# Feed-forward weights of a hybrid layer: split ahead of the stage, loaded two pairs ahead, with no pool border in between

## The chip, the cores and the metric

The kernel runs on one core of a Trainium2 chip. The metric is the time of one execution on the device, in microseconds; the figure of a kernel is the median over its runs. Five engines work side by side, each through its own instructions in order: TensorE (PE in the profile) does the matmuls, VectorE (DVE) and ScalarE (ACT) do elementwise work, GpSimd (POOL) little here, and SyncE (SP) issues nearly all transfers from device memory. An instruction starts when the one before it on its engine lets it and when the semaphores that it waits for have come.

## The reference, cut to what matters

The layer has a mixer (a gated delta rule and a differential attention), a cross attention to a memory, and a feed-forward stage. The change touches the end of the cross attention (its output projection) and the feed-forward stage:

```python
h = h + _mem_attn(_rmsnorm(h, p['ln_mem_q']), mem_k, mem_v, p['w_mem_q'], p['w_mem_o'])
hn = _rmsnorm(h, p['ln_ffn'])
h = h + jnp.square(jax.nn.relu(hn @ p['w_ff1'])) @ p['w_ff2']
...
y_prompt = _rmsnorm(hp, ln_final)
y_sample = _rmsnorm(hs, ln_final)
```

D_MODEL is 1024, D_FF is 4096, all in float32. The two request groups have 512 and 64 tokens, which the kernel carries side by side as T = 576 columns.

## The kernel before

**Number format.** Activations lie transposed: features on the 128 partitions, tokens along the row. A float32 factor is kept as a high part (a cast on ScalarE) and a low part (source minus high part, on VectorE), and a product takes three matmuls: high by high, high by low, low by high. `halves_to` (L1220) makes the two parts of an activation, `split_weights` (L155) and `split` (L1279) those of a weight tile. The splits of weights stand under a higher priority, so the scheduler puts them early in each engine's order.

**The output projection of the cross attention.** The loop at L1244 goes over the eight blocks of 128 output features in the order 0, 4, 1, 5, 2, 6, 3, 7. For a block it loads 128 columns of `w_mem_o` into a buffer `raw` (three of them), makes `wh` and `wl` (two of each), and `project` (L169) runs two halves of the tokens, 256 and 320 columns, each into a PSUM bank `pr` (three of them). `add_residual` (L1087) adds the bank to the residual `hT`, and squares it on ScalarE and adds the square to `accq` on VectorE for the norm of the next stage. After each block `combine` (L1224) scales the residual by the gain of the feed-forward norm and forms sums and differences of token halves and of the blocks m and m+4.

**The feed-forward stage.** The norm's factor is taken out of the product (the relu is homogeneous, the square makes it a factor of the second product's result), so the stage works on unnormalized features, and the factor `rB` is applied at the end. The first product is done in 16 pairs of 128-column blocks by a scheme with seven half-size products instead of eight: `ff1_pair` (L1294) loads a pair's weights as two tiles of 512 KB, forms four sums of them on VectorE (L1306, L1307, L1310, L1311), splits them (`a1`, `w12`, `a2`, `w34`, one buffer of each) and runs products 1, 5, 6, 2, 7, 3 and 4, each 12 matmuls of 288 columns, in PSUM banks `ba`, `gs` and `g1`. Products share banks: `keep` (L1342) copies a bank on ScalarE before the next product adds to it, and `put` (L1347) adds two products, takes relu and square and splits the result. Group g is two pairs; beside them run the eight blocks of the second product for group g-1, whose weights `w2` come in tiles of 256 KB. In the last group `last_weights` (L1397) loads and splits the weights of the last eight blocks in four tiles.

**What sets the order.** A scheduler orders each engine's instructions by priority and by when it expects a buffer to be free. Memory comes from pools with a fixed number of buffers for a name. After the loop at L1244 ten matmuls against a column of ones sum `accq` over the features (the norm), the pools `sp` and `wp` of all stages before are closed at L1254, and a new pool `fp` for the feed-forward stage is laid out in the memory that they leave (L1268). A buffer of `fp` waits for the tiles that lay there before.

## Time and profile before

| what | value |
|---|---|
| three runs | 1034.03, 1034.13 and 1035.53 us; median 1034.13 us |
| the profiled execution | 1033.64 us, of which 1031.9 us are the span from its first to its last instruction |
| PE busy | 1001.4 us, 97% of the span, in 6630 matmuls |
| PE's weight loads | 920.4 us, beside the matmuls |
| DVE busy | 701.0 us, 68% |
| ACT busy | 534.9 us, 52% |
| POOL busy | 56.8 us, 6% |
| read and written in device memory | 79.14 MB and 9.74 MB, 86 GB/s over the span |

The page divides the span into 40 slices; in its rows for PE nearly every slice has a 9, that is, 90% or more. The stretch that the change is about lies between 560 us (the end of the cross attention) and 650 us (the second group's start), and the feed-forward stage fills the rest, to 1000 us. [...]

### The profile page before, as it was taken

What the parts mean: (1) busy time and instruction counts of PE and PEld (TensorE: products, weight loads), DVE (VectorE), ACT (ScalarE), POOL (GpSimd) and SP (SyncE); (2) the same over time, 40 slices, a digit from 0 to 9 for tenths busy, and PEclk for the clock granted to TensorE, in tenths of its full rate; (3) what the DMA queues carried; (4) which work ended last, traced back from release to release, by engine and by line L of the source; (5) the groups of instructions that cost most, each with busy time, mean ns of one, the idle gap of its engine ahead of it and who ended that gap; (6) DMA issues with size and microseconds to landing.
All of it is one profiled execution on the core that took longest, in us unless ns stands there. A gap on an engine that the chain in (4) does not pass through costs nothing.

```text
span 1031.9 us, 17262 instructions
## 1 busy us (share of the span) xinstructions
PE 1001.4 (97%) x6630; PEld 920.4 (89%) x6630; DVE 701.0 (68%) x1511; ACT 534.9 (52%) x1152; POOL 56.8 (6%) x123
## 2 busy tenths in 40 slices
PE   9999999999999999999999998999999999999986
PEld 7989899998888877999997888999999999999976
DVE  6676784776666676565665778866666676777783
ACT  6654664333465665444454556754444545555434
POOL 3431010100000000000000000000000000000000
PEclk9999999999999999999999998999999999999999
DMA  7432320100322355523111304222323322222102
GB/s 216 129 100 85 109 60 25 39 21 22 104 67 65 121 175 182 165 83 110 55 42 42 103 1 143 92 86 89 93 83 93 101 83 83 82 83 83 53 30 92
DMA packets 121253, 89.98 MB, mean 87 GB/s; under 512 B 5506, under 2 KB 112128, under 8 KB 120660
## 3 DMA queue, kind: packets, MB, share of 16 engines
q1 hardware_dynamic: 120804, 88.24, 28.4%
q8 instruction: 52, 0.85, 0.3%
q10 hardware_dynamic: 368, 0.66, 0.2%
q14 instruction: 29, 0.24, 0.1%
HBM read 79.14 MB, written 9.74 MB: 86 GB/s over the span
## 4 chain that ended last, share of the span: by engine, by line
PE 77%; DVE 8%; DMA 4%; issue 3%; ACT 3%; POOL 2%; POOLq 0%; ACTq 0%; DVEq 0%; SPq 0%
PE pr L107 42%; PE g L107 14%; PE ba L107 9%; PE gs L107 8%; DMA r<-in_w_ff_dram 3%; PE ba L113 2%; PE g L113 2%; DVE w34l L1284 1%; DVE a2l L1284 1%; ACT w34h L1283 1%; DVE s L1307 1%; DVE s L1306 0%; DVE w2l L1284 0%; DVE wl L162 0%; DVE s L1310 0%
## 5 line engine op out<-in xcount | busy, mean ns | idle before, releaser
L107 PE MATMUL pr<-u,wh 128*128 128x320 f32 (+2 forms) x1240 | 328.3, 342 | 2.0 <-DVE p L323 1.1
L107 PE MATMUL pr<-u,wl 128*128 128x256 f32 (+1 forms) x816 | 227.9, 303 | 0.0
L107 PEld LDWEIGHTS pr<-u,wh 128*128 128x128 f32 x1240 | 211.5, 188 | 18.2 <-DVE p L323 1.3
L107 PEld LDWEIGHTS pr<-u,wl 128*128 128x128 f32 x816 | 149.3, 188 | 3.8 <-issue 0.7
L162 DVE TENSOR_TENSOR wl<-raw,wh 128x1024 fp32r<-128x1024 f32 x65 | 79.6, 1224 | 36.5 <-ACT wh L161 34.7
L107 PE MATMUL pr<-u,w2h 128*128 128x320 f32 (+1 forms) x384 | 97.4, 338 | 4.5 <-DVE u L1389 2.2
L161 ACT CAST wh<-raw 128x1024 fp32r<-128x1024 f32 x65 | 68.3, 1051 | 58.5 <-PE pr L107 52.7
L1283 ACT CAST w2h<-r 128x512 fp32r<-128x512 f32 x56 | 34.7, 621 | 95.1 <-PE pr L107 94.2
L107 PE MATMUL pr<-f,w2h 128*128 128x320 f32 (+1 forms) x288 | 73.2, 338 | 0.9 <-DVE u L1389 0.8
L107 PEld LDWEIGHTS pr<-u,w2h 128*128 128x128 f32 x384 | 64.9, 188 | 10.0 <-issue 4.0
L107 PE MATMUL pr<-u,w2l 128*128 128x256 f32 (+1 forms) x256 | 64.9, 294 | 0.0
L107 PEld LDWEIGHTS pr<-f,w2h 128*128 128x128 f32 x288 | 48.9, 188 | 5.5 <-issue 2.3
L107 PE MATMUL pr<-f,w2l 128*128 128x256 f32 (+1 forms) x192 | 48.7, 294 | 0.0
L107 PEld LDWEIGHTS pr<-u,w2l 128*128 128x128 f32 x256 | 46.9, 188 | 1.3
L1389 DVE TENSOR_TENSOR u<-u,pr 128x256 f32<-128x256 f32 x96 | 40.5, 451 | 10.6 <-PE pr L107 10.2
L208 POOL TENSOR_TENSOR tiny<-tiny,nhalf 128x1 f32<-128x1 f32 (+4 forms) x10 | 10.0, 1003 | 639.2 <-DVE tiny L1453 547.2
L1284 DVE TENSOR_TENSOR w12l<-s,w12h 128x1024 fp32r<-128x1024 f32 x16 | 19.6, 1225 | 35.7 <-ACT w12h L1283 35.7
L1284 DVE TENSOR_TENSOR w2l<-r,w2h 128x512 fp32r<-128x512 f32 x56 | 38.6, 689 | 7.1 <-ACT w2h L1283 6.9
L107 PE MATMUL pr<-wh,u 128*128 128x512 f32 x128 | 41.3, 402 | 0.0
L107 PEld LDWEIGHTS pr<-f,w2l 128*128 128x128 f32 x192 | 35.1, 188 | 1.1
L1092 DVE TENSOR_TENSOR u<-u,pr 128x256 f32<-128x256 f32 (+1 forms) x48 | 21.6, 453 | 19.9 <-PE pr L107 19.8
L457 DVE SCALAR_TENSOR_TENSOR p<-p,gcol,p 128x579 f32<-128x579 f32 x33 | 27.1, 822 | 9.0 <-ACT p L455 8.6
(454 smaller groups left out, 2283.8 us busy)
## 6 DMA issues: line engine op xcount, KB each, us to landing
r<-in_w_ff_dram SPq DMA_DIRECT2D x36, 512.0 KB
raw<-in_w_in_dram SPq DMA_DIRECT2D x28, 512.0 KB
r<-in_w_ff_dram SPq DMA_DIRECT2D x56, 256.0 KB
raw<-in_w_mem_k_dram SPq DMA_DIRECT2D x8, 512.0 KB
raw<-in_w_mem_v_dram SPq DMA_DIRECT2D x8, 512.0 KB
raw<-in_w_out_dram SPq DMA_DIRECT2D x8, 512.0 KB
raw<-in_w_mem_q_dram SPq DMA_DIRECT2D x8, 512.0 KB
raw<-in_w_mem_o_dram SPq DMA_DIRECT2D x8, 512.0 KB
```

The source lines that it names most:

```text
L107: i = nc.tensor.matmul(out, lhsT, rhs, start=start, stop=stop, skip_group_check=skip_group_check)
L113: i = nc.tensor.transpose(out, in_, ident[:n, :n])
L161: A.copy(wh, raw)
L162: V.tensor_tensor(wl, raw, wh.bitcast(F32), ALU.subtract)
L208: G.tensor_tensor(out, in_, bc(nhalf[: in_.shape[0], 0:1], list(in_.shape)), ALU.pow)
L457: V.scalar_tensor_tensor(yv[:, :n], cb[:, i : i + n], cwt[:, m, i : i + 1], yv[:, :n], ALU.mult, ALU.add)
L1092: V.tensor_tensor(hm, hm, b, ALU.add)
L1283: A.copy(wh, src)
L1284: V.tensor_tensor(wl, src, wh.bitcast(F32), ALU.subtract)
L1307: V.tensor_tensor(s12[:, 1], s12[:, 0], A11, ALU.subtract)
L1389: V.tensor_tensor(am, am, b, ALU.add)
```

## The change

The pool `sp` is closed ahead of the output projection's loop and `fp` opened there; `wp` moves to the outer level and stays open to the end. The scaled features and their sums, which lay in four names of `sp`, lie in one tile `mid` of `fp` now. The two first-product tiles of pair 0 are loaded after the fourth block of the loop and split between the other blocks (`split_first`); those of pair 1 are loaded after the loop. From then on `ff1_pair` of pair p ends with the split of pair p+1 and the load of pair p+2. The sums of weights overwrite the loaded tile instead of going to tiles of their own; the split tiles live under the names `wh`, `wl` and `w4`, one set of each, with other groupings than before: `wh` twice for products 1 and 5, one pair of `wl` for products 6 and 7, three `w4` for products 2 and 4 and for product 3. The loaded tiles share the three `raw` buffers with `w_mem_o` and with the four last loads. Squares and their sum move out of the loop into group 2 (some of the squares are scheduled earlier), and the norm's matmuls into group 3.

The multiplications on PE stay the same in number and shape. VectorE and ScalarE each have 18 instructions more, as splits of 1024 columns are divided into splits of 512.

```diff
-    wp = work.enter_context(tc.tile_pool(name="wp", bufs=2))
+    wp = ctx.enter_context(tc.tile_pool(name="wp", bufs=2))
...
+    work.close()
+    fp = ctx.enter_context(tc.tile_pool(name="fp", bufs=1, reuse_waits="tile"))
+    def ft(tag, shape, bufs, dt=F32):
+        return fp.tile(shape, dt, tag=tag, name=nm(tag), bufs=bufs)
+    mid = ft("f1", [P, 8, T], 1)
...
-        scaled[m] = x = small("kd" if m < 4 else "aT", [P, T])
+        k = m % 4
+        scaled[m] = x = mid[:, (0 if m < 4 else 4) + k % 2]
...
+        t12, t34 = (mid[:, i + k % 2].rearrange("p (j n) -> p j n", j=2) for i in (2, 6))
...
-    for m in (0, 4, 1, 5, 2, 6, 3, 7):
-        project(weights(w_mem_o[0], m * P), mo, add_residual(m, True))
+    def wtile(tag, shape, dt=F32R):
+        return wp.tile(shape, dt, tag=tag, name=nm(tag), bufs=3 if tag == "raw" else 2)
+    def load_pair(p):
+        raws[p] = raw = [wtile("raw", raw_, F32) for i in range(2)]
+        for i in range(2):
+            src = w_ff1[0, 512 * i : 512 * i + 512, 2 * P * p : 2 * P * (p + 1)]
+            nc.sync.dma_start(raw[i], src.rearrange("(k p) n -> p k n", p=P))
+    def split_pair(p):
+        a, b = raws.pop(p)
+        A11, A21, A12 = a[:, :, :P], a[:, :, P:], b[:, :, :P]
+        s1 = ft("s1", block_, 2)
+        parts[p] = ws = {}
+        with tc.high_priority() if p > 1 else ExitStack():
+            V.tensor_tensor(s1, A21, b[:, :, P:], ALU.add)
+            ws[1] = low_and_high(wtile("wh", wide_))
+            halves_to(*ws[1], A11)
+            ws[5] = low_and_high(wtile("wh", wide_))
+            halves_to(*ws[5], s1)
+            V.tensor_tensor(A21, A11, A21, ALU.subtract)
+            V.tensor_tensor(A11, s1, A11, ALU.subtract)
+            t = [wtile("wl", raw_) for _ in range(2)]
+            halves_to(*t, a)
+            ws[6], ws[7] = ([x[:, :, c : c + P] for x in t] for c in (0, P))
+            t = [ft("w4", raw_, 3, F32R) for _ in range(2)]
+            halves_to(*t, b)
+            ws[2], ws[4] = ([x[:, :, c : c + P] for x in t] for c in (0, P))
+            V.tensor_tensor(A12, A12, A11, ALU.subtract)
+            ws[3] = low_and_high(ft("w4", wide_, 3, F32R))
+            halves_to(*ws[3], A12)
+    def split_first():
...
+    for i, m in enumerate((0, 4, 1, 5, 2, 6, 3, 7)):
+        project(weights(w_mem_o[0], m * P), mo, add_residual(m, False))
         combine(m)
-    b = bank()
-    for t, (q0, n) in enumerate(QT):
-        mm(b[:, t : t + 1], accs[0][:, q0 : q0 + n], ones[:, 0:1])
...
-    work.close()
-    fp = ctx.enter_context(tc.tile_pool(name="fp", bufs=1, reuse_waits="tile"))
+        if i == 3:
+            load_pair(0)
+            split_first()
+    load_pair(1)
...
         put(1, N0, x[:, :NH], None)
+        if p + 1 < 2 * NG:
+            split_pair(p + 1)
+        if p + 2 < 2 * NG:
+            load_pair(p + 2)
...
-        raw = ft("r1", [P, 4, 2 * P], 2)
+        raw = wtile("raw", raw_, F32)
...
-    row_broadcast(squared, rB)
+    def square_block(m):
...
+            if g == 2:
+                with tc.issue_after(nc.cur_bb.bb.instructions[-1]):
+                    square_block(m)
+            if g == 3 and m == 0:
+                norm_rows()
```

`split_first` has the sums and splits of `split_pair` for pair 0, in buffers `w4`, `w2` and `r2` of the new pool. `square_block` has the two lines of `add_residual` that square and add, and `norm_rows` has the lines removed after the loop and the call of `row_broadcast`.

**The order, first place.** DVE at the end of the output projection, where the bank of the last half block (`pr`, 128x320) is added. L1237 to L1241 (before) and L1245 to L1249 (after) are sums of `combine`, L1222 and L1230 low parts. Before:

```order
L1092 TENSOR_TENSOR u_4538<-u_4538,pr_6592 128x320
L1110 TENSOR_TENSOR accq<-accq,zr_6618 128x320
L1251 TENSOR_SCALAR tiny_6639<-ba_6633 128x5
L1237 TENSOR_TENSOR p_1194_6560<-aT_6621,p_1194_6560 128x288
L1240 TENSOR_TENSOR an_6623<-aT_6621,kd_6556 128x288
L1222 TENSOR_TENSOR u_6095<-aT_6621,u_6095 128x576
L1222 TENSOR_TENSOR u_6096<-p_1194_6560,u_6096 128x288
L1241 TENSOR_TENSOR an_6623<-aT_6621,p_1194_6560 128x288
L1252 RECIPROCAL tiny_6640<-tiny_6639 128x5
L1222 TENSOR_TENSOR u_6097<-an_6623,u_6097 128x576
L1311 TENSOR_TENSOR s_1212_6653<-r_1207_6648 128x512
L1284 TENSOR_TENSOR a1l_6655<-r_1207_6648,a1h_6654 128x512
```

And now:

```order
L1230 TENSOR_TENSOR wl_6746<-raw_6611,wl_6745 128x1024
L1092 TENSOR_TENSOR u_4538<-u_4538,pr_6575 128x320
L1230 TENSOR_TENSOR wh_6740<-s_1204_6735,wh_6740 128x512
L1245 TENSOR_TENSOR f_1134_6104<-f_1134_6104 128x288
L1248 TENSOR_TENSOR f_1134_6104<-f_1134_6104 128x288
L1249 TENSOR_TENSOR f_1134_6104<-f_1134_6104 128x288
L1230 TENSOR_TENSOR u_6095<-f_1134_6104,u_6095 128x576
L1230 TENSOR_TENSOR u_6096<-f_1134_6104,u_6096 128x288
L1230 TENSOR_TENSOR u_6097<-f_1134_6104,u_6097 128x576
L1230 TENSOR_TENSOR w_1210_6750<-raw_6612,w_1209_6749 128x1024
L1374 TENSOR_TENSOR c_6674<-gs_6618,keep_6632 128x288
```

The norm's steps and the first pair's weight splits are gone from this place; splits of pair 1 stand between the rows of the last block, and the first output of pair 0 (L1374) follows.

**The order, second place.** ACT in the middle of a pair (the second pair of group 1), from the relu and square of the first output. The copy that product 4 needs, since it adds to the same bank, is the `keep` in these rows. Before:

```order
L1353 ACTIVATE c_7301<-c_7301 128x288
L1354 ACTIVATE c_7301<-c_7301 128x288
L1344 COPY keep_7319<-ba_7244 128x288
L1358 CAST f_1224_6665<-c_7301 128x288
L1283 CAST w34h_7509<-s_1350_7492 128x1024
L1353 ACTIVATE c_7333<-c_7333 128x288
```

And now:

```order
L1375 ACTIVATE c_7232<-c_7232 128x288
L1376 ACTIVATE c_7232<-c_7232 128x288
L1380 CAST f_1236_6906<-c_7232 128x288
L1229 CAST wl_7303<-raw_7047 128x1024
L1366 COPY keep_7250<-ba_7175 128x288
L1229 CAST w_1294_7307<-raw_7048 128x1024
```

The copy stood ahead of the cast of the output and of the next pair's weights; it stands behind both now.

**The order, third place.** DVE in the last group, behind the last pair, where PE runs blocks of the second product and their banks (`pr`) have to be added (L1389 and L1391, now L1415 and L1417). The rows of 1024 columns are low parts of the last weights. Before:

```order
L1409 TENSOR_TENSOR u_10634<-r_1855_10635,u_10633 128x1024
L1409 TENSOR_TENSOR u_10634<-r_1861_10672,u_10633 128x1024
L1359 TENSOR_TENSOR f_1781_10171<-c_10568,f_1781_10171 128x288
L1284 TENSOR_TENSOR w2l_10716<-r_1868_10713,w2h_10715 128x512
L1359 TENSOR_TENSOR f_1781_10171<-c_10575,f_1781_10171 128x288
L1356 TENSOR_TENSOR c_10594<-c_10594,rB_6661 128x288
L1389 TENSOR_TENSOR u_6952<-u_6952,pr_10606 128x256
L1389 TENSOR_TENSOR u_6952<-u_6952,pr_10617 128x320
L1359 TENSOR_TENSOR f_1781_10171<-c_10594,f_1781_10171 128x288
L1391 TENSOR_TENSOR u_6952<-u_6952,pr_10606 128x256
L1389 TENSOR_TENSOR u_6952<-u_6952,pr_10645 128x256
L1409 TENSOR_TENSOR u_10634<-r_1867_10709,u_10633 128x1024
```

And now:

```order
L1435 TENSOR_TENSOR u_10625<-raw_10626,u_10624 128x1024
L1435 TENSOR_TENSOR u_10625<-raw_10663,u_10624 128x1024
L1435 TENSOR_TENSOR u_10625<-raw_10700,u_10624 128x1024
L1331 TENSOR_TENSOR w2l_10707<-r_1824_10704,w2h_10706 128x512
L1381 TENSOR_TENSOR f_1753_10192<-c_10559,f_1753_10192 128x288
L1381 TENSOR_TENSOR f_1753_10192<-c_10566,f_1753_10192 128x288
L1378 TENSOR_TENSOR c_10585<-c_10585,rB_6615 128x288
L1415 TENSOR_TENSOR u_6905<-u_6905,pr_10597 128x256
L1415 TENSOR_TENSOR u_6905<-u_6905,pr_10608 128x320
L1435 TENSOR_TENSOR u_10625<-raw_10737,u_10624 128x1024
```

Three low parts stand in a row ahead of the first two banks now, where there were two.

More of the change, by code (lines that the diff above doesn't have):

```diff
@@ L1216, in hybrid_layer_kernel @@
     B1 = [cp.tile([P, 2, T], F32R, tag=f"qz{i}", name=nm("B1")).rearrange("p j (k t) -> p j k t", k=2) for i in range(2)]
+    work.close()
+    fp = ctx.enter_context(tc.tile_pool(name="fp", bufs=1, reuse_waits="tile"))
+    def ft(tag, shape, bufs, dt=F32):
+        return fp.tile(shape, dt, tag=tag, name=nm(tag), bufs=bufs)
+    block_, wide_, raw_ = [P, 4, P], [P, 2, 4, P], [P, 4, 2 * P]
+    mid = ft("f1", [P, 8, T], 1)
     scaled, steps = {}, {}
@@ L1224, in combine @@
     def combine(m):
-        scaled[m] = x = small("kd" if m < 4 else "aT", [P, T])
+        k = m % 4
+        scaled[m] = x = mid[:, (0 if m < 4 else 4) + k % 2]
         A.activation(x, hT[m // 4][:, m % 4, :], AF.Identity, scale=gcol[:, G_FF + m : G_FF + m + 1])
-        k = m % 4
+        t12, t34 = (mid[:, i + k % 2].rearrange("p (j n) -> p j n", j=2) for i in (2, 6))
         if m < 4:
             halves_to(*(B1[k // 2][:, j, k % 2, :] for j in range(2)), x[:, N0])
-            steps[k] = t12 = small("p0", [P, 2, NH])
             V.tensor_tensor(t12[:, 0], x[:, N1], x[:, N0], ALU.subtract)
@@ L1235, in combine @@
             return
-        top, t12, t34 = scaled[k], steps[k], small("an", [P, 2, NH])
+        top = scaled[k]
         V.tensor_tensor(t12[:, 1], x[:, N1], t12[:, 0], ALU.subtract)
@@ L1242, in combine @@
         halves_to(*(T34[j][:, :, k, :] for j in range(2)), t34)
-    for m in (0, 4, 1, 5, 2, 6, 3, 7):
-        project(weights(w_mem_o[0], m * P), mo, add_residual(m, True))
-        combine(m)
-    b = bank()
-    for t, (q0, n) in enumerate(QT):
-        mm(b[:, t : t + 1], accs[0][:, q0 : q0 + n], ones[:, 0:1])
-    cols, squared = tiny([P, 5]), tiny([P, 5])
-    V.tensor_scalar(cols, b[:, :5], 1.0 / D, EPS, ALU.mult, ALU.add)
-    V.reciprocal(squared, cols)
-    work.close()
-    fp = ctx.enter_context(tc.tile_pool(name="fp", bufs=1, reuse_waits="tile"))
@@ L1257, in hybrid_layer_kernel @@
-    laid = {}
-    def ft(tag, shape, bufs, dt=F32):
-        if tag in laid:
-            return laid.pop(tag)
-        return fp.tile(shape, dt, tag=tag, name=nm(tag), bufs=bufs)
+    def wtile(tag, shape, dt=F32R):
+        return wp.tile(shape, dt, tag=tag, name=nm(tag), bufs=3 if tag == "raw" else 2)
+    raws, parts = {}, {}
+    def load_pair(p):
[3 more added lines that the diff above has]
+            nc.sync.dma_start(raw[i], src.rearrange("(k p) n -> p k n", p=P))
@@ new lines, in low_and_high @@
+    def low_and_high(t):
+        return [t[:, 0], t[:, 1]]
+    def split_pair(p):
[20 more added lines that the diff above has]
+            halves_to(*ws[3], A12)
@@ new lines, in split_first @@
+    def split_first():
+        a, b = raws.pop(0)
+        A11, A21, A12, A22 = a[:, :, :P], a[:, :, P:], b[:, :, :P], b[:, :, P:]
+        s1 = ft("s1", block_, 2)
+        parts[0] = ws = {i: low_and_high(ft("w4", wide_, 3, F32R)) for i in (1, 5, 6)}
+        for i in (2, 7, 3):
+            ws[i] = [ft("w2" + x, block_, 3, F32R) for x in "hl"]
+        ws[4] = [ft("r2", block_, 3, F32R) for _ in range(2)]
+        V.tensor_tensor(s1, A21, A22, ALU.add)
+        halves_to(*ws[1], A11)
+        halves_to(*ws[5], s1)
+        V.tensor_tensor(A21, A11, A21, ALU.subtract)
+        V.tensor_tensor(A11, s1, A11, ALU.subtract)
+        halves_to(*ws[6], A11)
+        halves_to(*ws[2], A12)
+        halves_to(*ws[7], A21)
+        V.tensor_tensor(A12, A12, A11, ALU.subtract)
+        halves_to(*ws[3], A12)
+        halves_to(*ws[4], A22)
@@ L1264, in hybrid_layer_kernel @@
+    for i, m in enumerate((0, 4, 1, 5, 2, 6, 3, 7)):
+        project(weights(w_mem_o[0], m * P), mo, add_residual(m, False))
+        combine(m)
+        if i == 3:
+            load_pair(0)
+            split_first()
+    load_pair(1)
     temps = lambda n: ft("tm", [P, 320], 2)[:, :n]
     odd = lambda: ft("f1", [P, 2, 4, T], 1, F32R)
-    block_, wide_ = [P, 4, P], [P, 2, 4, P]
-    for tag, shape, bufs, dt in (
-        ("r1", [P, 4, 2 * P], 2, F32), ("keep", [P, NH], 4, F32), ("s12", wide_, 1, F32),
-        ("r2", block_, 3, F32), ("w2h", block_, 3, F32R), ("s34", wide_, 1, F32),
-        ("a1h", block_, 1, F32R), ("a1l", block_, 1, F32R), ("w12h", wide_, 1, F32R), ("w12l", wide_, 1, F32R),
-        ("a2h", [P, 4, 2 * P], 1, F32R), ("a2l", [P, 4, 2 * P], 1, F32R), ("w34h", wide_, 1, F32R),
-        ("rB", [P, T], 1, F32), ("c", [P, NH], 3, F32), ("tm", [P, 320], 2, F32), ("w34l", wide_, 1, F32R),
-        ("f1", [P, 2, 4, T], 1, F32R), ("w2l", block_, 3, F32R),
-    ):
-        laid[tag] = fp.tile(shape, dt, tag=tag, name=nm(tag), bufs=bufs)
@@ L1276, in hybrid_layer_kernel @@
-    f1 = odd()
     rB = ft("rB", [P, T], 1)
@@ L1294, in ff1_pair @@
     def ff1_pair(p, sx):
-        raw = []
-        for i in range(2):
-            raw.append(ft("r1", [P, 4, 2 * P], 2))
-            src = w_ff1[0, 512 * i : 512 * i + 512, 2 * P * p : 2 * P * (p + 1)]
-            nc.sync.dma_start(raw[i], src.rearrange("(k p) n -> p k n", p=P))
-        A11, A21 = raw[0][:, :, :P], raw[0][:, :, P:]
-        A12, A22 = raw[1][:, :, :P], raw[1][:, :, P:]
-        s12, s34 = (ft(tag, [P, 2, 4, P], 1) for tag in ("s12", "s34"))
-        with tc.high_priority():
-            V.tensor_tensor(s12[:, 0], A21, A22, ALU.add)
-            V.tensor_tensor(s12[:, 1], s12[:, 0], A11, ALU.subtract)
-        a11, ws12 = split(A11, "a1", 1), split(s12, "w12", 1)
-        with tc.high_priority():
-            V.tensor_tensor(s34[:, 1], A12, s12[:, 1], ALU.subtract)
-            V.tensor_tensor(s34[:, 0], A11, A21, ALU.subtract)
-        a2, ws34 = split(raw[1], "a2", 1), split(s34, "w34", 1)
-        def block(w, c):
-            return [x[:, :, c * P : (c + 1) * P] for x in w]
+        ws = parts.pop(p)
         def of(x, n):
@@ L1323, in ff1_pair @@
         operands = {
-            1: (a11, lambda j, k: B1[k // 2][:, j, k % 2, :]),
-            2: (block(a2, 0), half(B2, N0)),
-            3: ([x[:, 1] for x in ws34], half(B2, N1)),
-            4: (block(a2, 1), of(T34, 1)),
-            5: ([x[:, 0] for x in ws12], of(T12, 0)),
-            6: ([x[:, 1] for x in ws12], of(T12, 1)),
-            7: ([x[:, 0] for x in ws34], of(T34, 0)),
+            1: lambda j, k: B1[k // 2][:, j, k % 2, :], 2: half(B2, N0), 3: half(B2, N1),
+            4: of(T34, 1), 5: of(T12, 0), 6: of(T12, 1), 7: of(T34, 0),
         }
         def product(i, b, start):
-            w, x = operands[i]
+            w, x = ws[i], operands[i]
             for k in range(4):
@@ L1459, in hybrid_layer_kernel, with norm_rows @@
     ff1_pair(1, pend)
-    row_broadcast(squared, rB)
+    def square_block(m):
+        for a0, n in HALVES:
+            hm = hT[m // 4][:, m % 4, a0 : a0 + n]
+            if m == 0:
+                if a0 == 0:
+                    accs[0] = const([P, T], "accq")
+                A.activation(accs[0][:, a0 : a0 + n], hm, AF.Square)
+                continue
+            sq = temps(n)
+            A.activation(sq, hm, AF.Square)
+            ac = accs[0][:, a0 : a0 + n]
+            V.tensor_tensor(ac, ac, sq, ALU.add)
+    def norm_rows():
+        b = bank()
+        for t, (q0, n) in enumerate(QT):
+            mm(b[:, t : t + 1], accs[0][:, q0 : q0 + n], ones[:, 0:1])
+        cols, squared = tiny([P, 5]), tiny([P, 5])
+        V.tensor_scalar(cols, b[:, :5], 1.0 / D, EPS, ALU.mult, ALU.add)
+        V.reciprocal(squared, cols)
+        row_broadcast(squared, rB)
     accu[0] = (lambda u: [u[:, i] for i in range(2)])(pair(4))
     for g in range(1, NG):
-        nxt = (f1 if g == 1 else odd()) if g % 2 else pair(5, F32R)
+        nxt = odd() if g % 2 else pair(5, F32R)
         for m in range(KT):
```

## The prediction

> **What bounds the kernel now.** I read the page first: PE is busy for 97% of the span, so only what PE waits for, or does at a slower clock, can be won or lost. Then PE's timeline at the border of the feed-forward stage. Columns: start in us, length in us, engine, line, operation, names and shapes, number of matmuls, and in brackets the idle time before and what ended it.

> ```profile
> 617.24 0.83 PE L107 MATMUL ba<-ones,accq 128*128 128x1 f32 x6 [1.27 <-DVE accq L1110]
> 621.69 0.85 PE L107 MATMUL ba<-B,a1h 128*128 128x288 f32 x2 [3.62 <-ACT a1h L1283]
> 623.16 0.61 PE L107 MATMUL ba<-B,a1l 128*128 128x288 f32 x1 [0.63 <-DVE a1l L1284]
> 623.57 0.68 PE L107 MATMUL ba<-B,a1h 128*128 128x288 f32 x2
> ...
> 624.29 0.68 PE L107 MATMUL ba<-B,a1h 128*128 128x288 f32 x2
> ...
> 636.62 0.53 PE L107 MATMUL ba<-u,a2h 128*128 128x288 f32 x2 [1.00 <-ACT keep L1344]
> ...
> 638.32 0.42 PE L107 MATMUL ba<-B,a1h 128*128 128x288 f32 x2
> 638.58 0.29 PE L107 MATMUL ba<-B,a1l 128*128 128x288 f32 x1
> 638.71 0.43 PE L107 MATMUL ba<-B,a1h 128*128 128x288 f32 x2
> ```

> PE waits 1.27, 3.62, 0.63 and 1.00 us: for the last square's sum, for the first pair's weights (cast only behind everything of the last block), and for a copy behind pair 1's casts. Between, three matmuls take 0.72 us (623.57 to 624.29), and later 0.39 us (638.32 to 638.71). The windows say why. Columns: stretch, its length, busy time of PE, its weight loads, DVE, ACT and POOL with their instructions, granted clock, share of the transfer engines, GB/s.

> ```profile
> 610.00:620.00 10.00, 6.79 (x46) 6.35 (x45) 5.84 (x16) 4.68 (x9) 0.00 (x0) 0.90 0.00 0
> 620.00:625.00 5.00, 2.68 (x9) 2.34 (x10) 4.33 (x9) 3.29 (x5) 0.00 (x0) 0.50 0.52 153
> 625.00:630.00 5.00, 5.00 (x28) 5.00 (x28) 4.65 (x6) 3.43 (x6) 0.00 (x0) 0.67 0.79 229
> ```

> The clock is halved from 618.0 (0.90 over ten microseconds is two at half) to 628.3 (0.67 over five is 3.3 at half). The rest of the stage waits little: between 660 and 975 us the waits of PE are one line, seven times 0.2 us.

> ```profile
> PE pr L107 <- DVE u L1389: 1.3, 7, 0.2
> ```

> In the last group PE stops twice for banks that DVE hasn't added yet.

> ```profile
> 981.67 0.55 PE L107 MATMUL pr<-u,w2h 128*128 128x320 f32 x2 [1.70 <-DVE u L1389]
> ...
> 987.29 0.54 PE L107 MATMUL pr<-u,w2h 128*128 128x320 f32 x2 [2.21 <-DVE u L1391]
> ```

> **What the border gives back.** Pair 0's weights are split between the blocks of the projection, the norm's matmuls move to group 3 (the same ten, so their busy time moves and is not won), and the squares' sum leaves the last block. The four waits are 1.27 + 3.62 + 0.63 + 1.00 = 6.52 us. From 621.69 to 628.3 PE works 6.6 - 0.63 = 6.0 us at half clock, which at 0.39 in place of 0.72 us for three matmuls is 3.3 us: 2.7 us more. Together 9.2 us, if PE stays fed. What remains there is the last block's own chain. Its parts are these DVE rows and one ACT row; a product is 12 matmuls.

> ```profile
> 615.66 0.49 DVE L1092 TENSOR_TENSOR u<-u,pr 128x320 f32<-128x320 f32 x1 [1.49 <-PE pr L107]
> ...
> 616.69 0.49 DVE L1110 TENSOR_TENSOR accq<-accq,zr 128x320 f32<-128x320 f32 x1 [0.54 <-ACT zr L1105]
> ...
> 618.18 0.45 DVE L1237 TENSOR_TENSOR p<-aT,p 128x288 f32<-128x288 f32 x1
> 618.55 0.45 DVE L1240 TENSOR_TENSOR an<-aT,kd 128x288 f32<-128x288 f32 x1
> 618.92 0.75 DVE L1222 TENSOR_TENSOR u<-aT,u 128x576 fp32r<-128x576 f32 x1
> ...
> 621.82 0.69 DVE L1311 TENSOR_TENSOR s<-r 128x512 f32<-128x512 f32 x1
> 622.42 0.69 DVE L1284 TENSOR_TENSOR a1l<-r,a1h 128x512 fp32r<-128x512 f32 x1
> ...
> 628.43 1.23 DVE L1284 TENSOR_TENSOR w34l<-s,w34h 128x1024 fp32r<-128x1024 f32 x1
> ```
> ```profile
> 616.56 0.76 ACT L1228 ACTIVATE aT<-u,gcol 128x576 f32<-128x576 f32 x1
> ```
> ```profile
> 676.97 1.59 PE g L107 x12
> ```

> In the new order DVE has a 1024-column low part of pair 1 ahead of the last bank, then the add, ACT's scaling, three sums, two low parts: 1.23 + 0.49 + 0.76 + 3 x 0.45 + 0.75 + 0.45 = 5.0. DVE's rows overlap by 0.08 us (0.45 long, 0.37 apart), six times 0.5; with three handovers of 0.04 us it is 4.7 us. PE has 35 matmuls that don't need it (products 1 and 5, ten of product 6, one of 2): 35 x 0.1325 = 4.6 us. I take 0.25 us lost; between 0 and 1.2, if the low part waits for its buffer as well. The splits of pair 0 cost nothing, because they take the place of the squares: four sums and seven low parts of 512 columns, 0.60 us apart, are 6.6 us on DVE, and the squares' sums that leave the loop were seven blocks of two rows of up to 0.49, 6.4 us. With that cover gone DVE would run 6.6 us late, and the projection's banks with it.

> **What each pair pays.** In each pair ACT now has the copy that product 4 waits for behind the output's cast and the next pair's 1024-column cast of `wl`, which has to wait for product 7 to leave that buffer. Columns: number of instructions and least, median and most ns; then, in the groups by line, busy us and mean ns of one.

> ```profile
> L1344 ACT COPY keep<-ba x35: 381/392/403, 701.1 to 969.1; 128x288 f32<-128x288 f32 x35
> L1352 DVE TENSOR_TENSOR c<-gs,keep x11: 450/451/451, 706.0 to 947.4; 128x288 f32<-128x288 f32 x11
> ```
> ```profile
> L1354 ACT ACTIVATE c<-c 128x288 f32<-128x288 f32 x52 | 21.8, 442 | 0.8
> ...
> L1283 ACT CAST w34h<-s 128x1024 fp32r<-128x1024 f32 x13 | 13.7, 1057 | 5.7 <-PE g L107 5.7
> ...
> L1358 ACT CAST u<-c 128x288 fp32r<-128x288 f32 x24 | 9.7, 430 | 0.2
> ```
> ```profile
> 623.12 0.04 issue
> ```

> From product 2's end: sum 0.45, relu and square 0.44 each, cast 0.43, weight cast 1.06, copy 0.39, together 3.21; less 0.2 us by which ACT's casts overlap, plus five handovers of 0.04, plus 0.16 us by which the last matmul of a product outlives its slot (0.29 long, 0.13 apart): 3.37 us. PE covers it with products 7 and 3, 24 x 0.1325 = 3.18. So product 4 waits 0.2 us in each pair, where the copy stood first before and nothing waited. Bounds: 0 (with less handover) and 0.45 us, if the weight cast starts that much later for its in-place sum on DVE. Over pairs 2 to 15 this is 14 x 0.2 = 2.8 us (0 to 6.3). Pairs 0 and 1 get 0.4 each, 0.8 (0 to 2.0, the 1.00 us row twice), since their ACT has the unhurried split of pair 1 too. The 18 further instructions on DVE and ACT (a 1024-column part as two of 512 costs 2 x 0.60 in place of 1.13 us) lie in DVE's idle third:

> ```profile
> 700.00:800.00 100.00, 99.48 (x686) 95.77 (x684) 67.70 (x126) 48.50 (x100) 0.00 (x0) 1.00 0.29 88
> ```

> Transfers are as many as before and are issued earlier; the one line of waits above names none of them, so this wins nothing behind 660 us.

> **The last group.** Three low parts of the last weights stand in a row, where two did.

> ```profile
> 976.82 2.36 DVE L1409 TENSOR_TENSOR u<-r,u 128x1024 fp32r<-128x1024 f32 x2 [0.45 <-ACT u L1408]
> 979.10 0.45 DVE L1359 TENSOR_TENSOR f<-c,f 128x288 fp32r<-128x288 f32 x1
> ...
> 980.80 0.81 DVE L1389 TENSOR_TENSOR u<-u,pr 128x256 f32<-128x256 f32 x2
> ```

> Two take 2.36 - 1.23 = 1.13 us from start to start, so the banks are added 1.13 us later and the first stop grows from 1.70 to 2.8. The fourth low part stands alone behind it, and the next bank follows within the next half block of PE (12 matmuls of 320 columns, 12 x 0.1325 x 320/288 = 1.8 us); the second stop nearly vanishes (0.1). 3.91 becomes 2.9 to 3.1: 0.9 us won (-0.5 to 1.5).

> **The sum**, against the profiled execution (1033.64 us, 0.49 below the median of 1034.13): 1033.64 - 9.2 + 0.25 + 2.8 + 0.8 - 0.9 = **1027.4 us**.

> **The rivals.** *The clock falls in the last group.* One stop of 2.9 us is longer than either was. The clock stayed at 1.00 through stretches in which PE was half busy,

> ```profile
> 980.00:983.40 3.40, 1.73 (x12) 1.73 (x13) 3.33 (x9) 1.48 (x2) 0.00 (x0) 1.00 0.77 251
> 983.40:986.80 3.40, 1.68 (x10) 1.23 (x9) 3.10 (x5) 1.05 (x1) 0.00 (x0) 1.00 0.01 2
> ```

> and it fell at 618.0, behind a stretch in which PE had waited 1.27 us and done only one-column matmuls. A stop of 2.9 us lies between. If the clock falls for the same 10.3 us, PE loses (1 - 0.39/0.72) x 10.3 = 4.7 us, for two thirds of that time 3.1: 1030.5 to 1032.1, about 1031.4. [...] *No wait at product 4*: if handovers are shorter than I count, the 2.8 us aren't paid, 1024.6; for it speaks that 0.2 us is a small difference of large sums, against it that ACT runs in order. *Slower*: the cast of `wl` needs the in-place sum that overwrites the loaded tile, which DVE does behind that pair's own low parts; each 0.1 us that it comes later costs 1.4 us over 14 pairs. From 0.63 us later on, that is 0.83 us in a pair, the kernel is slower than before: 1036.2 at 0.63 + 0.2. Against it: DVE is 68% busy in the row for 700 to 800 us, so it isn't late for long. *The border stays*: the first products still find a weight or a sum missing for some 3.6 us, and the clock still halves: 9.2 becomes 2.9, 1033.7.

> **How the numbers follow.** Chances: forecast 0.43 (1025.8 to 1029.5), fallen clock 0.33, no wait at product 4 0.12, border stays 0.06, slower 0.06. The range from 1023.8 to 1033.0 holds the first three with the bounds of their terms. What a measurement of this kernel tells from no change is about 0.2%, 2.07 us. Faster by more than that (under 1032.06): the forecast, no wait, and nine tenths of the fallen clock, 0.84; within: 0.09; slower: 0.07.

> **What would show it.** Right: no wait of PE over 0.7 us between 570 and 650 us and a clock of 1.00 there; a wait of 0.2 us for `keep` (ACT) at product 4 of each pair; one stop of about 3 us in the last group. The granted clock behind that stop decides between 1027 and 1031. Wrong: waits of PE on `wl` or `raw` within the projection, waits of product 4 over 0.5 us, or a half clock before the last group.

## The result, and the profile after

The changed kernel takes 1027.16 us (median of four runs, 1026.13 to 1028.23). The kernel before, run beside it, takes 1034.83 us (1034.03 to 1035.61). The ratio is 0.9926 with an interval of 0.9909 to 0.9943: 7.7 us less, where the prediction said 1027.4 us and a range of 1023.8 to 1033.0. A second series on another occasion gave 1027.98 against 1035.31 us, 0.9933 (0.992 to 0.9945). The profiled execution of the first series took 1028.23 us, with a span of 1026.5 us; that of the second 1027.69 and 1026.0 us.

First the windows of the changed kernel around the old border (columns as in the prediction: PE, weight loads, DVE, ACT and POOL with their instructions, granted clock, share of the transfer engines, GB/s), then what PE waited for between 560 and 660 us (us in total, times, longest).

```profile
560.00:570.00 10.00, 7.60 (x36) 5.84 (x35) 4.90 (x18) 3.64 (x12) 0.00 (x0) 0.83 0.01 2
570.00:580.00 10.00, 9.70 (x59) 8.78 (x59) 6.67 (x14) 6.13 (x12) 0.00 (x0) 1.00 0.16 52
...
600.00:610.00 10.00, 10.00 (x67) 9.61 (x66) 7.70 (x16) 4.85 (x8) 0.00 (x0) 1.00 0.35 105
610.00:620.00 10.00, 10.00 (x70) 9.63 (x69) 8.29 (x18) 6.24 (x12) 0.00 (x0) 1.00 0.07 22
620.00:630.00 10.00, 10.00 (x76) 9.78 (x75) 8.27 (x14) 7.43 (x18) 0.00 (x0) 1.00 0.43 129
630.00:640.00 10.00, 9.50 (x70) 9.03 (x69) 6.90 (x14) 7.54 (x16) 0.00 (x0) 1.00 0.38 109
```
```profile
PE gs L107 <- ACT p L1181: 1.6, 1, 1.6
PE ba L107 <- ACT keep L1366: 0.9, 2, 0.5
```

Where PE was busy 2.68 of 5 us at half clock before (620 to 625 us), it is now busy throughout at full clock. Two waits for `keep`, 0.50 us at product 6 of pair 1 and 0.39 at product 4 of pair 2, are the longest that PE has there, under the 0.7 us that the prediction allowed; the 1.6 us belong to the attention, ahead of the change. The 0.83 of the first row is also there, and I come back to it at the end.

Now one pair of the stage: PE's and ACT's timelines around products 3 and 4 of the second pair of group 1.

```profile
672.57 1.76 PE L107 MATMUL g<-u,w 128*128 128x288 f32 x12
674.37 1.87 PE L107 MATMUL ba<-u,w 128*128 128x288 f32 x12
676.08 0.40 PE L107 MATMUL pr<-u,w2h 128*128 128x512 f32 x1
```
```profile
672.63 0.43 ACT L1380 CAST f<-c 128x288 fp32r<-128x288 f32 x1
672.98 1.04 ACT L1229 CAST wl<-raw 128x1024 fp32r<-128x1024 f32 x1
673.92 0.39 ACT L1366 COPY keep<-ba 128x288 f32<-128x288 f32 x1
```

Read starts, not busy times: twelve matmuls should take 1.59 us from start to start. Product 3 (`g`) takes 674.37 - 672.57 = 1.80 and product 4 (`ba`) 676.08 - 674.37 = 1.71. So 0.21 us go by before product 4 and 0.12 within it, although no row shows an idle time: the modelled ends of the matmuls cover gaps this small, and the list of PE's waits for 660 to 975 us is empty. What ended the gap is seen on ACT: the copy ends at 673.92 + 0.39 = 674.31, and product 4 starts 0.06 us later.

Last, the last group: PE's stop, the low parts on DVE ahead of it, and the window behind it.

```profile
977.27 0.90 PE L107 MATMUL pr<-u,w2h 128*128 128x320 f32 x2 [2.78 <-DVE u L1415]
```
```profile
971.28 3.50 DVE L1435 TENSOR_TENSOR u<-raw,u 128x1024 fp32r<-128x1024 f32 x3 [0.45 <-ACT u L1434]
974.70 0.68 DVE L1331 TENSOR_TENSOR w2l<-r,w2h 128x512 fp32r<-128x512 f32 x1
975.30 0.82 DVE L1381 TENSOR_TENSOR f<-c,f 128x288 fp32r<-128x288 f32 x2
976.03 0.45 DVE L1378 TENSOR_TENSOR c<-c,rB 128x288 f32<-128x288 f32 x1
976.40 0.81 DVE L1415 TENSOR_TENSOR u<-u,pr 128x256 f32<-128x256 f32 x2
```
```profile
975.00:980.00 5.00, 2.73 (x10) 2.73 (x11) 5.00 (x12) 1.56 (x3) 0.00 (x0) 0.68 0.03 9
```

One stop of 2.78 us, as forecast, behind three low parts in a row; and the clock did fall, for 3.4 us (0.68 over 5 us is 3.2 us at half, and 0.98 in the next 5 us is 0.2).

The time by place, worked out from the traces of both kernels and three of the experiments below: the start of the last matmul of product 4 of a pair, counted from the attention's last `gs<-u,kd` matmul, in us. "Changed" is the second series' execution.

```
pair   before  changed  copy first  split held back  squares back
  0     73.63    62.31       62.31            69.32         64.70
  3    121.68   110.37      109.60           116.86        114.38
  6    193.46   183.42      181.80           190.18        187.42
  7    217.68   210.01      207.86           216.74        211.78
 15    410.60   404.00      399.34           410.75        405.82
```

The norm's ten matmuls and the ten of its broadcast stand in pair 7 now, which takes 26.6 us where other pairs take 24.3; in the kernel before they are in the first rows. Setting these 2.3 us aside (their price in the changed kernel, taken for the kernel before as well), the border gave 11.31 - 2.3 = 9.0 us up to pair 3. From there to pair 15 the gain falls to 6.6 us: 2.4 us, or 0.2 us a pair, are given back. The last group gives back a little more: from that matmul to the first one of the last eight blocks it takes 17.13 us before and 17.40 us now.

### The profile page after: what moved, and what is told of

It reads as the page before. It is cut to its first block, busy times and chain, and to the rows that moved or that the text cites. A ratio compares the mean times of both kernels' runs of the same rounds, so it can differ in the third digit from the quotient of the medians.

```text
span 1026.5 us, 17294 instructions
## 1 busy us (share of the span) xinstructions
PE 1003.6 (98%) x6630; PEld 921.1 (90%) x6630; DVE 706.8 (69%) x1529; ACT 537.0 (52%) x1170; POOL 57.1 (6%) x123
## 4 chain that ended last, share of the span: by engine, by line
PE 84%; DVE 4%; issue 3%; ACT 3%; POOL 2%; DMA 1%; POOLq 0%; ACTq 0%; DVEq 0%; SPq 0%
PE pr L107 49%; PE g L107 14%; PE ba L107 10%; PE gs L107 7%; PE ba L113 2%; PE g L113 2%; DVE wl L162 0%; DMA raw<-in_w_ff_dram 0%; POOL tg L208 0%; DVE p L457 0%; DMA out_dram<-S 0%; DMA S<-in_state_gdn_dram 0%; POOL X L604 0%; DMA r<-in_w_ff_dram 0%; DVE on L780 0%
## 5 line engine op out<-in xcount | busy, mean ns | idle before, releaser
L107 PE MATMUL pr<-u,wh 128*128 128x320 f32 (+2 forms) x1240 | 328.2, 342 | 2.1 <-DVE p L323 1.0
L107 PEld LDWEIGHTS pr<-u,wh 128*128 128x128 f32 x1240 | 211.6, 188 | 18.6 <-DVE p L323 1.3
L107 PE MATMUL pr<-u,wl 128*128 128x256 f32 (+1 forms) x816 | 227.7, 303 | 0.0
L107 PEld LDWEIGHTS pr<-u,wl 128*128 128x128 f32 x816 | 149.7, 189 | 3.7 <-issue 0.7
L107 PE MATMUL pr<-u,w2h 128*128 128x320 f32 (+1 forms) x384 | 99.2, 343 | 2.8 <-DVE u L1415 2.8
L107 PE MATMUL pr<-f,w2h 128*128 128x320 f32 (+1 forms) x288 | 73.8, 340 | 0.0
L107 PEld LDWEIGHTS pr<-u,w2h 128*128 128x128 f32 x384 | 65.9, 191 | 7.9 <-DVE u L1415 3.1
L107 PE MATMUL pr<-u,w2l 128*128 128x256 f32 (+1 forms) x256 | 65.8, 298 | 0.0
L1415 DVE TENSOR_TENSOR u<-u,pr 128x256 f32<-128x256 f32 x96 | 42.9, 449 | 18.5 <-PE pr L107 17.6
L107 PE MATMUL ba<-u,wl 128*128 128x288 f32 x360 | 52.9, 295 | 0.6 <-ACT keep L1366 0.5
L107 PEld LDWEIGHTS pr<-f,w2h 128*128 128x128 f32 x288 | 48.7, 188 | 4.2 <-issue 1.2
L107 PEld LDWEIGHTS ba<-u,wl 128*128 128x128 f32 x360 | 49.2, 188 | 1.2 <-ACT keep L1366 1.2
L107 PEld LDWEIGHTS pr<-u,w2l 128*128 128x128 f32 x256 | 47.5, 191 | 1.5
L107 PE MATMUL pr<-f,w2l 128*128 128x256 f32 (+1 forms) x192 | 48.8, 295 | 0.0
L107 PE MATMUL pr<-wh,u 128*128 128x512 f32 x128 | 41.2, 400 | 0.0
L107 PEld LDWEIGHTS pr<-f,w2l 128*128 128x128 f32 x192 | 35.2, 188 | 1.1
L1375 ACT ACTIVATE c<-c 128x288 f32<-128x288 f32 x48 | 20.9, 442 | 28.1 <-DVE c L1374 28.1
```

The lines of the kernel that those rows point to most:

```text
L107: i = nc.tensor.matmul(out, lhsT, rhs, start=start, stop=stop, skip_group_check=skip_group_check)
L1375: A.activation(c, c, AF.Relu)
L1415: V.tensor_tensor(am, am, b, ALU.add)
```

## The experiments

The first is the base of all comparisons. They were run on four occasions, on which the kernel before took between 1033.31 and 1035.31 us, so across occasions the ratios to it compare better than the medians.

**The changed kernel again.** No edit.

> The changed kernel once more, as the base of the comparisons on this chip. Expected: 1027.2 us (1026 to 1028.3), as in its first runs, a stop of 2.8 us in the last group with one stretch of 3.4 us at half clock behind it, no wait over 2.0 us between 570 and 650 us. If the stretch at half clock seen at 563.7 us belongs to the kernel it shows again; if it comes from where the clock's windows happen to lie, it may be missing, and the time is then up to 0.9 us less.

1027.98 us (1027.23 to 1029.4). The stop of 2.78 us and the stretch at half clock behind it are there; the stretch at 563.7 us isn't, and the span is 0.5 us shorter. So that one doesn't belong to the change.

**The border, 1: the split written late.**

```diff
-        if i == 3:
-            load_pair(0)
-            split_first()
+    load_pair(0)
+    split_first()
     load_pair(1)
```

> Load and split of pair 0 are written behind the whole loop of the output projection, without the pool border. Theory 'border' (what cost the time was that the new pool lay in memory that the last block still used; the scheduler places the split early by itself where memory is free): within 1 us of the changed kernel, 1026 to 1028, no wait over 1 us at pair 0. Theory 'place' (the gain comes from writing the split into the middle of the loop): waits of 3.6 and 0.6 us at pair 0 come back, and the half clock with them, 5 to 7 us more, 1032 to 1034.

1028.22 us, ratio to the kernel before 0.9937 (0.9923 to 0.995): the same as the changed kernel within the intervals. PE's longest waits at the first pairs are 0.38, 0.56 and 0.65 us. By the starts, writing the split into the middle of the loop is worth 1.2 us at pair 3 (111.57 here, 110.37 in the changed kernel); the span of its profiled execution, 1025.5 us, hides it, since there is no half clock in its last group. ACT's casts of the split stand between 596 and 616 us, ahead of the last block, though they are written behind it. So the place in the text explains 1.2 of the 9.0 us, which speaks for the theory "border"; a kernel with the pool border alone put back was not run.

**The border, 2: the split held back.**

```diff
         if i == 3:
             load_pair(0)
-            split_first()
+    with tc.issue_after(nc.cur_bb.bb.instructions[-1]):
+        split_first()
```

> Pair 0 is loaded early as in the changed kernel, but its split is held behind the last block of the projection. By the terms of the prediction (waits of 3.62 and 0.63 us, and 2.7 us for the half clock behind them): a wait of 3.5 to 5 us at pair 0's first product and 5 to 8 us more than the changed kernel, 1032 to 1035, with half clock for about 10 us behind the wait. Rival: the split's time is hidden anyway since ScalarE's casts run ahead and products 1 and 5 need only a part of it: a wait under 2 us, no half clock, 1 to 2 us more.

1034.24 us, ratio 0.9995 (0.9985 to 1.0005): nearly all of the gain is gone. PE's timeline and the window there (the first row is product 1 of pair 1, which the scheduler put ahead of the wait):

```profile
615.77 1.75 PE L107 MATMUL ba<-B,wh 128*128 128x288 f32 x12
621.76 2.77 PE L107 MATMUL ba<-B,w 128*128 128x288 f32 x10 [4.24 <-DVE w L1230]
624.33 1.88 PE L107 MATMUL g<-u,w 128*128 128x288 f32 x12
```
```profile
620.00:625.00 5.00, 3.24 (x15) 3.24 (x16) 5.00 (x9) 2.26 (x4) 0.00 (x0) 0.66 0.00 0
```

A wait of 4.24 us for the low part of the first weight, as expected; ten matmuls that take 2.57 us (start to start) where 1.33 would do; but the half clock lasts 3.4 us (0.66 over 5 us) and not the 10 us of the kernel before. In the table the price is 116.86 - 110.37 = 6.5 us at pair 3. The mechanism holds; the length of the slow stretch was carried over from the kernel before and was wrong.

**The border, 3: squares and norm back.** `add_residual(m, True)` in the loop, the norm's matmuls behind it, `square_block` and `norm_rows` gone.

> The changed kernel with the squares, their sum and the norm's ten matmuls back in the output projection and right behind it, as before; pair 0 is still split between the blocks and there is no pool border. By the prediction (the splits lie in the time that the squares leave; with that cover gone DVE is 6.6 us late and the banks of the projection with it): waits in the projection of several us and 1.3 us at the norm, 3 to 8 us more than the changed kernel, 1030 to 1035. Rival (DVE has room for both): only the wait for the last square's sum, 1.3 us, less the 0.9 us that the ten matmuls cost in group 3, so within 1 us of the changed kernel.

1029.1 us, ratio 0.9948 (0.9933 to 0.9963), which alone doesn't part it from the changed kernel. The trace does: 211.78 - 210.01 = 1.8 us at pair 7, behind which both have done the norm. PE's waits between 600 and 641 us:

```profile
601.84 0.56 PE L107 MATMUL pr<-u,wh 128*128 128x320 f32 x2 [0.60 <-DVE u L1092]
```
```profile
640.38 0.79 PE L107 MATMUL ba<-u,w 128*128 128x288 f32 x4 [1.33 <-ACT keep L1372]
```

DVE is not 6.6 us late with splits and squares both in the loop; one bank is 0.6 us late. The wait of 1.33 us is for the copy ahead of product 4 of pair 1, and the 1.3 us that were expected at the norm's matmuls do not appear. The cover that the prediction named for the splits (that they take the squares' place) was not needed for most of them.

**The pair, 1: the copy ahead of the cast.**

```diff
         product(7, x, False)
-        s3 = keep(x)
+        with tc.high_priority():
+            s3 = keep(x)
```

> The copy of bank ba before product 4 stands ahead of the cast of wl on ScalarE, nothing else. Theory 'copy' (the copy behind the cast costs 0.2 us a pair, 14 pairs, and a little more in pairs 0 and 1): 2.2 to 3.6 us less than the changed kernel, about 1024.2, and the excess of 0.2 us between products 3 and 4 is gone from the starts of the matmuls. Theory 'elsewhere' (the 2.6 us given back between 640 and 960 us come from the weights of the second product or from the norm): no difference, within 0.5 us of the changed kernel.

1022.56 us, ratio 0.9875 (0.986 to 0.989): 5.4 us less than the changed kernel, more than either theory allowed. PE and ACT in the second pair of group 2:

```profile
719.16 1.76 PE L107 MATMUL g<-u,w 128*128 128x288 f32 x12
720.76 1.76 PE L107 MATMUL ba<-u,w 128*128 128x288 f32 x12
722.36 0.39 PE L107 MATMUL pr<-f,w2h 128*128 128x512 f32 x1
```
```profile
719.56 0.39 ACT L1366 COPY keep<-ba 128x288 f32<-128x288 f32 x1
719.85 1.05 ACT L1229 CAST wl<-raw 128x1024 fp32r<-128x1024 f32 x1
```

The copy ends 0.81 us before product 4 needs it, and both products take 1.60 us. From pair 3 to pair 15 this kernel wins 4.66 - 0.77 = 3.9 us over the changed one, 0.32 a pair. To see where, add up in these twelve pairs by how much each distance between two starts of PE exceeds the usual one of its shape, leaving out excesses under 0.035 us: the changed kernel loses 5.9 us in this way and this one 1.7. Of the 4.2 us between them 3.1 are product 4's (0.2 us, and 0.1 at the matmul behind it, in ten of the twelve pairs). Most of the rest is at banks of the second product, which come late less often here.

It wins over the kernel before there as well: that one is 12.08 us behind at pair 3, of which 2.3 are the norm's matmuls, and 11.26 at pair 15, so 11.26 - 9.78 = 1.5 us. The kernel before had been waiting in these pairs too, 4.2 us by the same count. (Some go the other way, 0.8 us in the changed kernel and 1.2 in this one: distances under that limit are a little longer there, 0.235 in place of 0.231 us behind a matmul of 512 columns. Why was not tried.) Its timeline shows where it waited, once in nearly every pair, 0.3 to 0.5 us each time: three matmuls of the second product take 0.84 us, where two of 0.15 and one of 0.23 would do, since DVE's sum of a bank comes late.

```profile
719.22 1.00 PE L107 MATMUL pr<-f,w2h 128*128 128x320 f32 x3
720.06 0.27 PE L107 MATMUL pr<-f,w2l 128*128 128x256 f32 x1
```

**The pair, 2: the copy made twice, behind the cast.** In the changed kernel:

```diff
         product(7, x, False)
+        A.copy(temps(NH), x[:, :NH])
         s3 = keep(x)
```

> The changed kernel with a second copy of the same bank (128 x 288, result unused) right ahead of the copy that product 4 waits for, behind the cast of wl. Theory 'copy' (PE has no slack left there, so all that ScalarE does between product 7 and the copy is waited for): each pair's product 4 starts later by the time of one copy, 0.35 to 0.39 us; 14 to 16 pairs make 5 to 6 us more than the changed kernel, 1033 to 1034. Theory 'fixed price' (the 0.3 us at product 4 is what a handover at this bank costs, whatever stands in the queue): no difference, 1027.5 to 1028.5.

1025.87 us, ratio 0.9918 (0.99 to 0.9936): not 5 us more but, if anything, less. Both theories missed. The rows of the second pair of group 2 say why:

```profile
718.86 1.76 PE L107 MATMUL g<-u,w 128*128 128x288 f32 x12
720.47 0.39 PE L107 MATMUL pr<-f,w2h 128*128 128x512 f32 x1
720.70 0.28 PE L107 MATMUL pr<-f,w2l 128*128 128x256 f32 x1
720.96 1.86 PE L107 MATMUL ba<-u,w 128*128 128x288 f32 x12
```
```profile
720.50 0.40 ACT L1366 COPY keep<-ba 128x288 f32<-128x288 f32 x1
```

The order on PE is another one: two matmuls of the second product stand between products 3 and 4 and fill the time. Product 4 still starts 0.06 us after the copy's end (720.90), as in the changed kernel; only 0.14 us of it are idle now, since 0.35 us of work lie in front. So the copy decides the start, and what this costs depends on what else PE is given there. That the scheduler put them there because it reckoned with the longer queue is an argument, not a measurement.

**The pair, 3: the copy made twice, ahead of the cast.** The same second copy, inside the higher priority of the first experiment on the pair.

> The same second copy in the kernel where the copy stands ahead of the cast of wl. Theory 'copy' (there the cast's 1.06 us are no longer in front, so a slack of about 0.8 us is left): no wait at product 4, within 0.7 us of that kernel, 1022 to 1023.3. If product 4 waits for a copy all the same, 5 us more, about 1028.

1024.81 us, ratio 0.9912 (0.9894 to 0.9929), 2.3 us more than that kernel by the medians and 3.8 by the ratios. Product 4 doesn't wait (product 3 starts at 719.30, product 4 at 720.90), as the theory says, but the time was expected within 0.7 us and isn't: eight starts at banks of the second product are 0.1 to 0.4 us late, and the half clock behind the last group's stop lasted 6.8 us in this execution. A change in one queue again moved other work.

**The pair, 4: sums of banks first.** In the changed kernel, groups 0 to 5.

```diff
-            V.tensor_tensor(am, am, b, ALU.add)
+            with tc.high_priority() if g < NG - 2 else ExitStack():
+                V.tensor_tensor(am, am, b, ALU.add)
```

> The changed kernel with the sums of the second product's banks at the higher priority in groups 0 to 5, the last group untouched and the copy still behind the cast. Theory: two separate waits are paid in the stage, the copy before product 4 (0.2 us and 0.1 at the next matmul, 11 to 14 pairs) and once in a group the bank of the second product, whose sum DVE has behind low parts (0.14 us and 0.08, nine times, 1.9 us). Here the second kind goes and the first stays: 1 to 2 us less than the changed kernel, 1025.5 to 1027, product 4 still 0.2 us late in each pair. Rival (both come from the cast of wl, and the bank is late because of the copy): the starts at the banks stay late, no gain within 0.5 us.

1025.22 us, ratio 0.9913 (0.9892 to 0.9934). In the trace it wins 2.0 us over the changed kernel between pairs 0 and 15, and the late starts at product 4 stay in ten pairs, as expected. So product 4's wait does not hang on the banks' one. The other way round they are not quite apart: with the copy ahead the banks' late starts shrank too, from 2.6 to 1.6 us by the count above. The wait that goes here is this (it comes about once in a pair, not once in a group), in the changed kernel of the second series: five matmuls of product 1 are followed by the second half of a block that starts late, at 705.11 where 704.94 was due. The bank's sum on DVE, behind a low part, ends at 704.95, and the half block starts 0.15 us behind it, as at the other late banks.

```profile
704.28 0.82 PE L107 MATMUL ba<-B,wh 128*128 128x288 f32 x5
705.11 0.53 PE L107 MATMUL pr<-f,w2h 128*128 128x320 f32 x2
```
```profile
703.94 0.69 DVE L1331 TENSOR_TENSOR w2l<-r,w2h 128x512 fp32r<-128x512 f32 x1
704.54 0.41 DVE L1417 TENSOR_TENSOR u<-u,pr 128x256 f32<-128x256 f32 x1
```

**The last group, 1: low parts unhurried.** On top of the copy ahead.

```diff
         with tc.high_priority():
             A.copy(hi, src)
-            V.tensor_tensor(lo, src, hi.bitcast(F32), ALU.subtract)
+        V.tensor_tensor(lo, src, hi.bitcast(F32), ALU.subtract)
```

> On top of the copy moved ahead: the low parts of the last weights lose their higher priority, so that DVE has one of them ahead of the first bank of the last group and one behind it, the other two later. Theory 'last group' (the stop is the time of the low parts that stand in a row ahead of the bank, 1.13 us each, and the half clock comes only behind a stop near 2.8 us): the stop shrinks from 2.78 to between 0.5 and 1.7 us and the clock stays at 1.00 behind it: 2.5 to 3.8 us less than with the copy alone (1022.6), about 1019.5. Rival (DVE is full there, so that whatever is moved is waited for at the next bank or at the last blocks): the stops sum up to 2.5 to 3 us again, no gain from the waits, at most 1.6 us from the clock.

1020.3 us, ratio 0.9858 (0.9844 to 0.9873): 2.3 us less than with the copy alone (1.8 by the ratios), just under what was expected. PE's stop in the last group:

```profile
970.18 0.54 PE L107 MATMUL pr<-u,w2h 128*128 128x320 f32 x2 [1.69 <-DVE u L1418]
```

2.78 became 1.69, and the clock stays at 1.00 in all windows behind it. 1.1 us of wait and about 1.6 us of half clock went.

**The last group, 2: sums first.** On top of the copy ahead, the sums at the higher priority for g = 6.

> The copy ahead of the cast, and in the last group the sums of banks get the same higher priority as the low parts of the last weights, so DVE takes a bank's sum behind each low part. Theory 'last group': the stop of 2.78 us falls apart into shorter ones, each under 1.2 us, together 1 to 2 us, with the clock at 1.00: 1019 to 1021, as with the low parts unhurried (1020.3). Rival (the sums of outputs that now come later hold up the last blocks): a stop of over 1.5 us behind the pair's output, 1021 or more.

1019.64 us, ratio 0.986 (0.9843 to 0.9878), the same as the one before. The stop falls into two:

```profile
969.80 0.50 PE L107 MATMUL pr<-u,w2h 128*128 128x512 f32 x1 [0.58 <-DVE u L1417]
981.76 3.40 PE L107 MATMUL pr<-f,u 128*128 128x512 f32 x18 [1.13 <-DVE u L1094]
```

Together 1.71 us against 1.69 (and 0.19 more at the last blocks there): it looks as if DVE has that much work there whichever way it is ordered, and what it puts off is waited for at the last blocks. The half clock goes in both.

**The best of all.** All copies of a pair ahead of ACT's casts, and the sums first in the last group.

> All copies of a pair ahead of ScalarE's casts, and in the last group the sums of banks at the higher priority. Theory: with both waits of the stage and the stop of the last group taken away, the time is at most that of the copy ahead with the sums first in the last group alone (1019.6), 1018 to 1020. Rival (casts that are pushed back behind three copies come late for the next pair's first products): waits on wh or w4 at product 1 or 5, 1 to 3 us more than that.

1019.15 us (1018.93 to 1020.33), ratio 0.9852 (0.983 to 0.9875). It beats both kernels of the case, the kernel before by some 14 us, and can't be told from the two experiments above it. No wait on `wh` or `w4` at products 1 or 5 appeared.

**Loads one pair ahead.** `load_pair(p + 1)` at the start of `ff1_pair(p)`, and no load behind it.

> The changed kernel with each pair's weights loaded one pair ahead instead of two; the splits stay where they are. By the prediction (transfers win nothing behind 660 us): within 1 us of the changed kernel, 1027 to 1029. Rival (with one pair ahead a load ends too late for the split, which then stands in front of product 1): waits on wh or raw at each pair, over 0.3 us each, 4 us or more in all.

1027.44 us, ratio 0.9929 (0.9917 to 0.9941): no difference. PE's starts lie within 0.25 us of the changed kernel's through the stage. Loading two pairs ahead in place of one wins nothing.

## Why the prediction was right, and where it was right by luck

**What bounds the kernel.** Right in the main: the result was found as waits of PE and stretches at half clock, but for 0.7 us of the border and 0.8 us of slightly longer distances, named below.

**The border, 9.2 us less 0.25.** With the first four pairs' prices (0.8 and 0.4) the sum had 7.75 us up to pair 3; 9.0 were measured. The held-back split puts 6.5 us of it on the first weights and the squares 1.8 on squares and norm; 0.7 us stay unassigned. The last block's chain cost what was said: product 6 of pair 0 starts 0.15 us late and its next matmul 0.11, 0.26 for 0.25. Two other reasons of the step were weak. The cover named for the splits wasn't what held them, and 10.3 us at half clock are what the kernel before had, not what a late first weight always brings (3.4 us when it was held back).

**0.2 us a pair, 2.8 in all.** Net right: 2.4 us over twelve pairs, 0.2 each. Gross it was luck, errors that cancel. The mechanism was the predicted one, a copy behind the cast of `wl` that ends just too late, and 0.21 us is the forecast wait; but the matmul behind the late one pays another 0.1, so that ten pairs paid 3.1 us. What the sum left out lies at the banks of the second product: the kernel before lost 4.2 us there in these pairs and the changed one 2.6, which is 1.6 won, and 0.8 go to the slightly longer distances. 3.1 - 1.6 + 0.8 = 2.3, beside the 2.4 of the table. The row `PE pr L107 <- DVE u L1389: 1.3, 7, 0.2`, quoted to show that the rest of the stage waits little, has a third of the 4.2 us. The 0.8 us for pairs 0 and 1 fell elsewhere than said: nothing at product 4 of pair 0, the 0.50 us at product 6 of pair 1, 0.2 at its product 4 (read from the starts) and 0.39 at product 4 of pair 2, all for copies.

**The last group, 0.9 us less.** The stops went from 3.91 to 2.78 us, 1.1 won, as forecast. The rival "the clock falls" came true as well, at a third of its assumed length: 3.4 us at half, 1.6 us lost. It ate the gain: the group takes 0.3 us more than before, 17.40 us, and 16.0 in each of the three kernels with this stop that kept the clock there (squares back, split written late, sums first in groups 0 to 5). That a stop of 2.9 us keeps the full clock, as the forecast had it, was the author's estimate; of the ten stops of 2.8 us in the profiles three kept it. The forecast and this rival are therefore not alternatives here, and the distance of 4 us between them was too large.

**The sum.** Border 1.25 us better than said, last group 1.2 us worse, pairs as said: the total is right because these two cancel. The forecast stands 6.2 us under the profiled execution of the kernel before; the two profiled executions of the changed kernel lie 5.4 and 5.9 us under it, and the medians of kernels run side by side 7.7 and 7.3 us apart.

**The other rivals.** "No wait at product 4" and "the border stays" fell by the rows above. "Slower", a cast of `wl` that waits for its in-place sum, didn't happen: in the pair shown the cast starts 0.35 us after the one before it (672.98 against 672.63), without an idle time.

## What to carry to other kernels

Where PE is busy all the time, read distances between starts and not idle times: waits of 0.1 to 0.4 us that recur in each round mostly don't appear in the list of waits, and they made more here (5.9 us in twelve pairs of the changed kernel) than the visible stops. Before costing a new wait at "n times 0.2", look for the small waits that the same place pays already, since the change moves those too. And an instruction on whose end the busiest engine waits belongs ahead of long work on its own queue that nobody needs yet: one line of priority was worth as much here as two thirds of the whole change (5.4 us against 7.7).

## What the runs showed of the hardware

```profile
977.49 0.56 PE L107 MATMUL pr<-u,w2h 128*128 128x320 f32 x2 [2.78 <-DVE u L1414]
```
```profile
975.00:980.00 5.00, 2.52 (x15) 2.34 (x16) 5.00 (x11) 1.78 (x3) 0.00 (x0) 1.00 0.13 44
```

The stop of 1.57 us in the attention was followed by such a piece in the first profile of the changed kernel (the 0.83 above) and in the one with sums first in groups 0 to 5, and in no other.

The traces show what goes with it. In these profiles all times between two changes of the clock are whole multiples of 3.413 us (the stretches of the changed kernel's first profile last 3.413, 409.60, 3.413 and 40.96 us, that is 1, 120, 1 and 12 of them, those of the kernel before 10.24 and 399.36 us, 3 and 117), so the changes give a grid of windows for each profile. Where the stop of 2.8 us lost the clock, 2.19 to 2.79 us of it lay within one window (2.33 in the changed kernel's first profile, from 974.49 us to the fall of the clock at 976.82); in the three profiles that kept the clock a border cut it, and the larger part was 1.81, 1.59 and 1.45 us. The stop of 1.57 us lay whole within one window in five of fourteen profiles; two of these five lost the clock, and none of the other nine. What decides among the five is open, and no run moved a stop against the grid on purpose. At half clock three matmuls of 288 columns took 0.72 us (623.57 to 624.29 us in the kernel before), at full clock 0.39 (638.32 to 638.71), so each piece cost about 1.6 us (an estimate from these two times); the five runs of the changed kernel in the second series lie 2.2 us apart. Of the ten stops of 2.8 us seven lost the clock, of the fourteen of 1.57 us two.

The second thing is the 0.12 us at the matmul after a late one: twelve matmuls of product 4 take 1.71 us when its start was held up and 1.60 when it wasn't. Why was not tried.
